# Gate-and-up block product: weight sums made by adding transfers from GpSimd's queue, and every channel tile finished in its own stage

## The chip, the cores and the metric

One core of one Trainium2 chip runs the whole program. The metric is device time in microseconds of one launch. PE is TensorE (PEld its weight loads), DVE VectorE, ACT ScalarE, POOL GpSimd, SP SyncE; L12 is line 12 of the kernel.

## The reference

One layer of a diffusion step on 128 context rows and 1024 latent rows (1152 in all) of width 1024, in float32: a normalised and modulated input, an input projection, an HGRN2 scan and an RWKV-7 scan in two directions, an output projection, then a gated feed-forward part whose gate is convolved over the grid:

```python
def block(x, mod, s_hgrn, s_rwkv, ffn_conv_fn, p):
    ...
    x = x + gate1 * (jnp.concatenate([o_a, o_b], axis=-1) @ p['w_out'])
    h = rmsnorm(x, p['norm_ffn_w']) * (1 + scale2) + shift2
    gt = ffn_conv_fn(h @ p['ffn_w_gate']) + p['ffn_conv_b']
    x = x + gate2 * ((jax.nn.gelu(gt) * (h @ p['ffn_w_up'])) @ p['ffn_w_down'])
```

The gate and up weights are 1024 x 2816 each (22 channel tiles of 128), the down weight 2816 x 1024. The convolution is 3 x 3 over the latent grid and 3 wide over the context.

## The kernel before, in words

**Precision.** Every large product is made of three passes of the fast float32 format: a float32 operand is split into a high part (a cast on ACT) and a low part (a subtraction on DVE, which reads the high part), and PE adds high x high, high x low and low x high (`split`, `product`, `three`).

**Stages.** First norms, transposes and the modulation; then input projections, the two scans and the output projection, mixed; then the gate-and-up products with the convolution (`weights`, `front`, `ffn_front`, `ffn_mid`); then the down projection in two halves of eleven channel tiles each (`ffn_down`), the first half starting from channel tiles 0 to 10, the second from 11 to 21.

**The block product.** For a channel tile, gate and up together are one matrix product of 2 x 2 blocks, done by seven block products instead of eight, in the manner of Strassen and Winograd. The seven left-hand blocks (`hq`) are made once from the activations. The seven weight blocks are made for each channel tile in `weights(ft)` from the four quarters b11, b21 (gate, upper and lower half of the rows) and b12, b22 (up): b11, b21, b11+b12+b22, b11+b12, b22+b12, b11+b12+b22+b21, b22. Four of them need an addition of 128 x 512 elements, on DVE into a tile `tq` (L2095, by `combine`). Each is then split into a pair `fwh`, `fwl` (L2090); there are four buffers of each. The activations stand in two groups, "a" (320 columns) and "b" (256), and each pair serves both; a block product is twelve matmuls (L2120). The results are collected in three PSUM tiles (`sy`, `sx`, `sz`) and put into the gate row `raw` and the up tile `u` (L2158 to L2179).

**Weight buffers.** The gate columns of a tile come into `wr` (512 KB, one buffer), the up columns into `fru` (512 KB, one buffer), both from SP's queue (L2085).

**The channel tile's middle.** `ffn_mid` runs the convolution: on ACT the middle tap and the activation function (L2203, L2204, L2213), on DVE eight taps of 1024 elements (L2209) and two of 128, then three products with `u`, and the result is stored to `d_a` (L2219).

**Tiles put off.** For the last five channel tiles (`NLATE = 5`) `raw` and `u` are stored to HBM instead (`d_gt`, `d_up`, L2241 and L2242). `late(j)`, called inside the first half of the down projection, loads them again (L2255, L2256) and runs `ffn_mid` there.

**What sets the order.** The kernel records every operation, and `Plan.schedule` then puts them into one order per engine by a list schedule: of the operations that are ready, the one with the longest way to the end is taken, plus its lead. The lead is a number for the function it was recorded in (`LEADS`) and one from the table `NUDGE`. A store may be put on POOL's queue or SP's (`st`, `either`), loads are on SP's (`ld`). Each engine then runs its instructions strictly in that order.

Of the kernel before, what the change touches and what calls it, by code (L numbers as in the profile page):

```python
# [20 lines left out]
P = 128  # L21
# [10 lines left out]
NLATE = 5  # L32
# [15 lines left out]
NUDGE = {1: 6, 3: -7, 4: -41, 5: -2, 7: 9, 8: 9, 9: 9, 10: 9, 11: 20, 12: 19, 13: 19, 14: 15, 15: 15, 16: 5, 17: -4, 18: -1, 19: -4, 20: -18, 21: -29, 22: -19, 23: -26, 24: -26, 25: -6, 27: -3, 28: -3, 29: -3, 30: -3, 31: -5, 32: -3, 33: -3, 35: -3, 51: -5, 52: -5, 53: -2, 84: -6, 85: -6, 86: -6, 87: -6, 88: 6, 91: -3, 92: -6, 93: -6, 94: -6, 95: -6, 96: -6, 97: -6, 98: -6, 104: -7, 105: -4, 108: -6, 109: 4, 110: -6, 111: -6, 119: 6, 127: -7, 140: 6, 141: 6, 142: 6, 143: 21, 144: 6, 145: 6, 147: -2, 172: -17, 173: -17, 174: -17, 175: -17, 183: -14, 184: -20, 185: -4, 189: 57, 190: 57, 191: 69, 193: 5, 194: 3, 200: -15, 201: -8, 203: 11, 204: 14, 206: 3, 212: -16, 217: 13, 218: 5, 224: -48, 225: -15, 226: -15, 227: -15, 236: 7, 239: -2, 243: -26, 244: -26, 245: -26, 246: -19, 247: -26, 251: 7, 252: 7, 253: 5, 254: -12, 266: -4, 269: 3, 275: 61, 282: -16, 290: -9, 292: 2, 294: 18, 295: 18, 296: 18, 297: 28, 298: 28, 299: 28, 300: 48, 301: 48, 302: 30, 303: 27, 305: 30, 306: 30, 307: 30, 308: 37, 309: 40, 310: 40, 311: 40, 312: 51, 313: 42, 314: 47, 315: 43, 316: 23, 317: 26, 318: 26, 319: 23, 320: 23, 321: 23, 322: 23, 323: 22, 328: 10, 329: 13, 330: 29, 331: 29, 337: -10, 338: -10, 339: -10, 340: -10, 341: -10, 342: -10, 343: -10, 344: 10, 345: 10, 346: 5, 347: 8, 348: 8, 349: 8, 350: 11, 351: 8, 352: -12, 353: -14, 354: -8, 355: -14, 356: 15, 357: -2, 358: 33, 359: 7, 360: -4, 361: 4, 362: -3, 363: -4, 364: 7, 365: -7, 367: 13, 368: 23, 370: 25, 377: 6, 378: 13, 379: 13, 380: 18, 381: 18, 382: 18, 390: 1, 396: 6, 398: 5, 400: -10, 401: -10, 404: -6, 405: -6, 406: -6, 407: -6, 408: -6, 409: -6, 410: -6, 411: -6, 412: -6, 413: -2, 416: -23, 417: 3, 418: 3, 419: 3, 425: -3, 426: -3, 427: -3, 428: -3, 453: -3, 454: -3, 455: -5, 456: 20, 457: 5, 458: 20, 459: 3, 460: -15, 461: 1, 462: -4, 463: -11, 464: -4, 465: -4, 466: -4, 467: -4, 468: -4, 469: -2, 470: 32, 471: 15, 472: 15, 473: 16, 474: 1, 475: 1, 476: 15, 477: 10, 478: 14, 479: 15, 480: 28, 481: 10, 482: 12, 483: 34, 484: 24, 485: 26, 486: 6, 487: 21, 488: 6, 489: 11, 490: 20, 491: 13, 492: 25, 493: 2, 494: -16, 495: -5, 496: -5, 497: -5, 498: -5, 499: -43, 500: -20, 501: -18, 502: -16, 503: -39, 504: -13, 505: -12, 506: -12, 507: -15, 508: -36, 509: -37, 510: -24, 511: -24, 512: -38, 516: 21, 517: 22, 518: 22, 519: 11, 520: 11, 521: 11, 522: 1, 523: 11, 524: 1, 525: 11, 526: 9, 527: 26, 528: -1, 529: 1, 530: -5, 532: -34, 533: -34, 534: -26, 535: -27, 536: 8, 537: 22, 538: 22, 539: 45, 540: 16, 541: 18, 542: 14, 543: 14, 544: 4, 545: 13, 546: 4, 547: 4, 548: 53, 549: 39, 550: 39, 551: 52}  # L48
# [129 lines left out]
class Plan:  # L178
# [3 lines left out]
    HELPERS = ("mm", "st", "copy", "combine", "split", "load_w", "record", "either")  # L182
# [7 lines left out]
    def __init__(self, tc, base):  # L190
        nc = tc.nc
        self.base = {F32: base, F32R: base.bitcast(F32R), I32: base.bitcast(I32)}
        self.tc = tc
        self.units = {"PE": nc.tensor, "DVE": nc.vector, "ACT": nc.scalar, "POOL": nc.gpsimd, "SP": nc.sync}
        self.ops, self.tags, self.tiles = [], {}, [None]
        self.live, self.group, self.chain_end, self.lead, self.boxes = {}, None, {}, 0.0, []
        self.first, self.mark = None, 0
        Plan.last = self
# [81 lines left out]
    @staticmethod  # L280
    def operands(m, args, kw):

        isap = lambda x: isinstance(x, AP)
        w = [args[0]]
        r = [x for x in args[1:] if isap(x)]
        for k, x in kw.items():
            if isap(x):
                (w if k == "accum_out" else r).append(x)
        if (m == "matmul" and not kw.get("start", True)) or m == "copy_predicated":
            r.append(args[0])  # L290
        return w, r
# [34 lines left out]
    def close(self, forms, room=()):  # L326
# [51 lines left out]
        op.place, op.dense, op.lead, op.kind = None, False, self.lead + LEADS.get(self.kind, 0.0) + NUDGE.get(op.id // 16, 0), self.kind  # L378
# [11 lines left out]
        return op  # L390

# [50 lines left out]
    def cost(self, e, l):  # L442
# [11 lines left out]
        if m == "dma_start":  # L454
            return .45 if len(a[0].ap) < 3 and len(a[1].ap) < 3 else .68
# [363 lines left out]
def step_kernel(ctx: ExitStack, tc: tile.TileContext, I, O):  # L819
# [8 lines left out]

    tl = plan.tile
# [101 lines left out]
    Layout(hbm, 0, 10240).add("qb1", 1024, 10)  # L931
    for t, box in (("fwh", "wh"), ("fwl", "wl")):
        plan.tag(t, [(m, 512 * b) for m, _ in plan.tags[box].places for b in range(2)], 512)
# [7 lines left out]
    Layout(low, 4944, 9198).add("u2", T).add("araw", 1408)  # L941
# [224 lines left out]
    gtd = dram("d_gt", [NLATE, P, 1320])  # L1166
    upd = dram("d_up", [NLATE, P, T])
# [912 lines left out]
    def weights(ft):  # L2080

        c = slice(ft * P, (ft + 1) * P)
        wg, wu = tl("wr", [P, KT, P]), tl("fru", [P, KT, P])
        for w, n in ((wg, "gate"), (wu, "up")):
            ld(w, I["ffn_w_" + n][0][:, c].rearrange("(a p) n -> p a n", p=P))  # L2085
        b11, b21, b12, b22 = wg[:, 0:4], wg[:, 4:8], wu[:, 0:4], wu[:, 4:8]
# [6 lines left out]
        def total(a, b):  # L2093
            t = tl("tq", [P, 4, P])
            combine(t, a, b, ADD)  # L2095
            return t

        yield pair(b11)
        yield pair(b21)
        t1 = total(b11, b12)  # L2100
        t2 = total(t1, b22)
        yield pair(t2)
        yield pair(t1)
        yield pair(total(b22, b12))
        yield pair(total(t2, b21))
        yield pair(b22)
# [45 lines left out]
    def front(sb, raw, us):  # L2152
# [13 lines left out]
        for dst, c in gate_places(raw, sb, 0):  # L2166
            dve.tensor_tensor(dst, like(dst, x[:, c]), like(dst, keep[1][:, c]), ADD)
        product(2, (yield), y, sb, False)
        save(2)
        z = pbank("sz")  # L2170
        product(3, (yield), z, sb, True)
# [49 lines left out]
    for ft in range(NFT):  # L2221
# [16 lines left out]
        if ft < NFT - NLATE:  # L2238
            ffn_mid(ft, raw, us[0])
        else:  # L2240
            st(gtd[ft - NFT + NLATE], raw)  # L2241
            st(upd[ft - NFT + NLATE], us[0])  # L2242

# [6 lines left out]

    def late(j):

        ft = NFT - NLATE + j
        raw, u = graws[ft % 2], tl("u2", [P, T])
        ld(raw, gtd[j])  # L2255
        ld(u, upd[j])  # L2256
        ffn_mid(ft, raw, u)
# [67 lines left out]
    def ffn_down(half):  # L2325
# [9 lines left out]
        for k in ks:  # L2335
# [8 lines left out]
            if half == 0 and k % 2 and k // 2 < NLATE - 1:  # L2344
                late(k // 2)
        for j, i in enumerate(head):
            finish(half, i, dn[j], fnw)
        for i in rest:
# [11 lines left out]
            if half == 0 and i == 3:  # L2360
                late(NLATE - 1)
# [34 lines left out]
```

## Time and profile before

| what | us |
|---|---|
| time, median of 3 runs | 1822.85 (1821.17 to 1830.99) |
| span of the profiled execution | 1818.9 |
| PE busy | 1768.3 (97%) |
| DVE busy | 1415.1 (78%) |
| ACT busy | 862.0 (47%) |
| POOL busy | 289.3 (16%) |
| DMA, mean | 169 GB/s, 307.45 MB |

The profile is of one execution; the median of the runs is 3.95 us above its span. A row of the wait list says who waited for whom, the total in us, how often, and the longest. In a list of lines by form, the number after the bar is the busy time, then the mean in ns, then the idle time just before and what ended it. "Landing" is the time from the issue of a transfer to its last completion count.

### The profile page before, as it was taken

The numbers are of one execution on the slowest core, as the hardware profiler recorded it, in microseconds if no ns is written. First come the engines' busy times: TensorE is split into PE (matmuls) and PEld (weight loads), VectorE is DVE, ScalarE is ACT, GpSimd is POOL, SyncE is SP. The second block draws the span as 40 slices with busy tenths as digits, with TensorE's granted clock in tenths as the row PEclk, the third lists the DMA queues.
The fourth block names the chain that finished last, engine by engine and source line by source line (L and its number), as shares of the span: only waits on it lengthen the run. The fifth ranks groups of instructions, "written<-read, shape, count | busy, mean of one in ns | idle before, by whom it ended". The sixth has DMA issues, their size and how long they took to land.

```text
span 1818.9 us, 45180 instructions
## 1 busy us (share of the span) xinstructions
PE 1768.3 (97%) x18402; PEld 1587.1 (87%) x18402; DVE 1415.1 (78%) x2670; ACT 862.0 (47%) x1753; POOL 289.3 (16%) x553
## 2 busy tenths in 40 slices
PE   7999999999999999999999999999999999999998
PEld 5889888899888788888788799999999999888887
DVE  7559899887778888876867889999999954985543
ACT  6556656543255645643636754444444433321321
POOL 2013435353312222122110100000000000000000
PEclk9999999999999999999999999999999999999999
DMA  9325637487757568889967522222222247774451
GB/s 325 102 72 151 147 102 180 128 229 193 207 165 246 165 203 258 267 283 306 324 207 244 203 59 73 73 73 73 73 73 73 76 126 251 227 272 162 133 169 67
DMA packets 272176, 307.45 MB, mean 169 GB/s; under 512 B 62611, under 2 KB 216849, under 8 KB 271968
## 3 DMA queue, kind: packets, MB, share of 16 engines
q1 hardware_dynamic: 245584, 224.33, 41.3%
q0 software_dynamic: 26384, 80.23, 13.1%
q8 instruction: 144, 2.36, 0.5%
q14 instruction: 64, 0.52, 0.1%
HBM read 200.50 MB, written 103.99 MB: 167 GB/s over the span
## 4 chain that ended last, share of the span: by engine, by line
PE 69%; DMA 5%; DVE 3%; ACT 1%; issue 1%; POOL 0%; SPq 0%; DVEq 0%; ACTq 0%; POOLq 0%
PE banks L2120 27%; PE banks L2269 5%; PE banks L2270 5%; PE banks L2271 5%; PE banks L1125 3%; PE banks L1127 3%; PE banks L1126 3%; DMA low<-d_ak 2%; PE banks L2011 2%; PE banks L2013 2%; PE banks L2012 2%; PE banks L1776 1%; PE banks L1827 1%; PE banks L1846 1%; PE banks L1646 1%
## 5 line engine op out<-in xcount | busy, mean ns | idle before, releaser
L1125 PE MATMUL banks<-hh,wh 128*128 128x384 f32 x768 | 282.0, 367 | 0.7 <-DVE fx L1314 0.7
L1127 PE MATMUL banks<-hh,wl 128*128 128x384 f32 x768 | 259.0, 337 | 0.0
L1126 PE MATMUL banks<-hl,wh 128*128 128x384 f32 x768 | 258.7, 337 | 0.0
L2209 DVE SCALAR_TENSOR_TENSOR low<-low,pf 128x1024 f32<-128x1024 f32 x176 | 224.8, 1279 | 4.6 <-ACT low L2203 3.0
L2120 PE MATMUL banks<-qm,wh 128*128 128x320 f32 x968 | 223.3, 310 | 0.0
L2120 PE MATMUL banks<-hbm,wh 128*128 128x256 f32 x880 | 164.4, 283 | 1.3 <-ACT low L1991 1.3
L1125 PEld LDWEIGHTS banks<-hh,wh 128*128 128x128 f32 x768 | 144.9, 189 | 21.0 <-issue 11.4
L2120 PE MATMUL banks<-qm,wl 128*128 128x320 f32 x528 | 162.8, 308 | 0.0
L2120 PEld LDWEIGHTS banks<-qm,wh 128*128 128x128 f32 x968 | 160.7, 189 | 0.1
L1126 PEld LDWEIGHTS banks<-hl,wh 128*128 128x128 f32 x768 | 145.5, 189 | 2.4 <-issue 1.2
L1127 PEld LDWEIGHTS banks<-hh,wl 128*128 128x128 f32 x768 | 145.0, 189 | 0.0
L2120 PEld LDWEIGHTS banks<-hbm,wh 128*128 128x128 f32 x880 | 140.4, 191 | 1.7 <-ACT low L1991 1.7
L2120 PE MATMUL banks<-ham,wh 128*128 128x256 f32 (+1 forms) x616 | 132.4, 295 | 0.0
L2120 PE MATMUL banks<-hbm,wl 128*128 128x256 f32 x440 | 124.8, 284 | 0.0
L2120 PEld LDWEIGHTS banks<-ham,wh 128*128 128x128 f32 x616 | 102.2, 192 | 0.0
L2120 PEld LDWEIGHTS banks<-qm,wl 128*128 128x128 f32 x528 | 99.1, 188 | 0.0
L2269 PE MATMUL banks<-qm,hbm 128*128 128x512 f32 (+1 forms) x240 | 93.7, 390 | 0.0
L2270 PE MATMUL banks<-qm,hbm 128*128 128x512 f32 (+1 forms) x240 | 93.6, 390 | 0.0
L2271 PE MATMUL banks<-qm,hbm 128*128 128x512 f32 (+1 forms) x240 | 93.5, 390 | 0.0
L2090 ACT CAST wh<-fx 128x512 fp32r<-128x512 f32 x88 | 54.3, 620 | 80.6 <-PE banks L2120 76.0
L2158 ACT COPY fx<-banks 128x320 f32<-128x320 f32 (+1 forms) x132 | 52.0, 397 | 84.2 <-PE banks L2120 82.8
L2120 PEld LDWEIGHTS banks<-hbm,wl 128*128 128x128 f32 x440 | 84.4, 192 | 0.0
(527 smaller groups left out, 4333.5 us busy)
## 6 DMA issues: line engine op xcount, KB each, us to landing
wr<-in_w_in_dram SPq DMA_DIRECT2D x34, 512.0 KB, 5.6
d_a<-low POOLq DMA_DIRECT2D x22, 576.0 KB, 3.4
low<-d_ak SPq DMA_DIRECT2D x64, 192.0 KB, 4.4
low<-in_ffn_w_up_dram SPq DMA_DIRECT2D x22, 512.0 KB
wr<-in_ffn_w_gate_dram SPq DMA_DIRECT2D x22, 512.0 KB, 3.7
low<-d_kb SPq DMA_DIRECT2D x36, 256.0 KB, 5.3
low<-d_a SPq DMA_DIRECT2D x12, 704.0 KB, 4.6
low<-in_ada_w_dram SPq DMA_DIRECT2D x32, 256.0 KB, 6.0
```

Of the source, the lines that this page charges most:

```text
L1125: mm(o, wh[:, kt, :], hh[:, kt, c], kt == 0, False)
L1126: mm(o, wh[:, kt, :], hl[:, kt, c], False, False)
L1127: mm(o, wl[:, kt, :], hh[:, kt, c], False, kt == KT - 1)
L2011: mm(ps, oh[:, kt, :], woh, kt == 0, False)
L2012: mm(ps, oh[:, kt, :], wol, False, False)
L2090: split(*w, src)
L2120: pe.matmul(o, a[:, kt, :], b[:, kt, :], start=start and first, stop=last, skip_group_check=not start)
L2158: act.copy(keep[n], y[:, 0:w])
L2209: dve.scalar_tensor_tensor(av, shifted(dy, dx), tap(3 * dy + dx), av, MUL, ADD)
L2269: mm(o, lh, w[:, 0, c], first, False)
L2270: mm(o, lh, w[:, 1, c], False, False)
L2271: mm(o, ll, w[:, 0, c], False, last)
```

## The change

It does three things.

1. `weights(ft)` loads the four quarters one by one (256 KB each, tag `fw`, four buffers: two in `wr`, two in `fru`). The sums are not made on DVE any more: a transfer issued from POOL's queue adds a quarter from HBM onto a buffer in place (`acc`, with `accum_op=ADD`). One buffer t holds b11, then b11+b12, then b11+b12+b22, then b11+b12+b22+b21, and is split between the additions; a second, t3, holds b12+b22. Products 2 and 3 change places, because b11+b12 now exists before b11+b12+b22.
2. `NLATE`, `late`, `d_gt` and `d_up` are gone: all 22 channel tiles run `ffn_mid` right after their product.
3. The table `NUDGE` is drawn anew, and is looked up by function and by the count of that function's operations instead of by the operation's number.

```diff
-NLATE = 5
...
-NUDGE = {1: 6, 3: -7, 4: -41, ...}
+NUDGE = {'step_kernel': [1, 8, 104, ...], 'const': [102], ...}
...
-        if (m == "matmul" and not kw.get("start", True)) or m == "copy_predicated":
+        if (m == "matmul" and not kw.get("start", True)) or m == "copy_predicated" or "accum_op" in kw:
...
-... self.lead + LEADS.get(self.kind, 0.0) + NUDGE.get(op.id // 16, 0), self.kind
+... self.lead + LEADS.get(self.kind, 0.0) + self.nudge(self.kind), self.kind
...
+    def acc(out, src):
+        pool.dma_start(out, src, accum_op=ADD)
...
+    fru = plan.tags["fru"].places[0][1]
+    plan.tag("fw", [(plan.tags["wr"].places[0][0], 512 * b) for b in range(2)] + [(low, fru + 512 * b) for b in range(2)], 512)
...
-        wg, wu = tl("wr", [P, KT, P]), tl("fru", [P, KT, P])
-        for w, n in ((wg, "gate"), (wu, "up")):
-            ld(w, I["ffn_w_" + n][0][:, c].rearrange("(a p) n -> p a n", p=P))
-        b11, b21, b12, b22 = wg[:, 0:4], wg[:, 4:8], wu[:, 0:4], wu[:, 4:8]
+        quarter = lambda n, h: I["ffn_w_" + n][0][512 * h:512 * h + 512, c].rearrange("(a p) n -> p a n", p=P)
+        b11, b21, b12, b22 = quarter("gate", 0), quarter("gate", 1), quarter("up", 0), quarter("up", 1)
+        def fetch(src):
+            w = tl("fw", [P, 4, P])
+            ld(w, src)
+            return w
...
-        def total(a, b):
-            t = tl("tq", [P, 4, P])
-            combine(t, a, b, ADD)
-            return t
-        yield pair(b11)
-        yield pair(b21)
-        t1 = total(b11, b12)
-        t2 = total(t1, b22)
-        yield pair(t2)
-        yield pair(t1)
-        yield pair(total(b22, b12))
-        yield pair(total(t2, b21))
-        yield pair(b22)
+        t = fetch(b11)
+        yield pair(t)
+        acc(t, b12)
+        yield pair(fetch(b21))
+        yield pair(t)
+        acc(t, b22)
+        t3 = fetch(b12)
+        acc(t3, b22)
+        yield pair(t)
+        acc(t, b21)
+        yield pair(t3)
+        yield pair(t)
+        yield pair(fetch(b22))
...
+        z = pbank("sz")
+        product(3, (yield), z, sb, True)
         product(2, (yield), y, sb, False)
         save(2)
-        z = pbank("sz")
-        product(3, (yield), z, sb, True)
...
-        if ft < NFT - NLATE:
-            ffn_mid(ft, raw, us[0])
-        else:
-            st(gtd[ft - NFT + NLATE], raw)
-            st(upd[ft - NFT + NLATE], us[0])
+        ffn_mid(ft, raw, us[0])
...
-            if half == 0 and k % 2 and k // 2 < NLATE - 1:
-                late(k // 2)
...
-            if half == 0 and i == 3:
-                late(NLATE - 1)
```

Three places in the order. The new kernel's line numbers are 11 to 13 higher around here (the products are L2133 there, the transposes L2036, the splits L2104, the taps L2222, the store of a finished tile L2232), and 1 higher in the down projection.

POOL in the gate-and-up stage, before: stores alone (d_a is a finished tile, d_gt and d_up one that is put off).

```order
L2110 MEMSET low 128x1320
L2219 DMA d_a<-low 128x1152 x16
L2241 DMA d_gt<-low 128x1320
L2242 DMA d_up<-low 128x1152
L2219 DMA d_a<-low 128x1152
L2241 DMA d_gt<-low 128x1320
```

POOL in the same stage now, some five tiles into it: L2109, L2112 and L2116 are the three additions onto t, L2114 the one onto t3.

```order
L2109 DMA low<-in_ffn_w_up_dram 128x4x128
L2114 DMA wr<-in_ffn_w_up_dram 128x4x128
L2112 DMA low<-in_ffn_w_up_dram 128x4x128
L2116 DMA low<-in_ffn_w_gate_dram 128x4x128
L2109 DMA low<-in_ffn_w_up_dram 128x4x128
L2114 DMA low<-in_ffn_w_up_dram 128x4x128
L2232 DMA d_a<-low 128x1152
L2112 DMA low<-in_ffn_w_up_dram 128x4x128
L2116 DMA low<-in_ffn_w_gate_dram 128x4x128
L2109 DMA wr<-in_ffn_w_up_dram 128x4x128
```

A queue of stores has become a queue of additions, four per tile, and of the 22 stores of finished tiles 12 stay between them while 10 are on SP's queue.

PE where the products of the second group begin, before: the transposes are of the last two row tiles (0 and 7), wh and wl are the weight pairs, qm holds left-hand blocks of group "a", ham and hbm those of "b".

```order
L2120 MATMUL banks<-qm,wh_131 128x320 x2
L2120 MATMUL banks<-qm,wl_133 128x320
L2025 MATMUL banks<-c_ident,low 128x128 x8
L2120 MATMUL banks<-qm,wh_131 128x320 x2
L2120 MATMUL banks<-qm,wl_133 128x320
L2025 MATMUL banks<-c_ident,low 128x128 x8
L2120 MATMUL banks<-hbm,wh_131 128x256 x2
L2120 MATMUL banks<-hbm,wl_133 128x256
L2120 MATMUL banks<-hbm,wh_131 128x256 x2
```

PE at the same place now:

```order
L2133 MATMUL banks<-qm,wh_130 128x320 x2
L2133 MATMUL banks<-qm,wl_132 128x320
L2036 MATMUL banks<-c_ident,low 128x128 x16
L2133 MATMUL banks<-ham,wh_129 128x256 x2
L2133 MATMUL banks<-ham,wl_131 128x256
L2133 MATMUL banks<-ham,wh_129 128x256 x2
L2133 MATMUL banks<-ham,wl_131 128x256
L2133 MATMUL banks<-qm,wh_130 128x320 x2
L2133 MATMUL banks<-qm,wl_132 128x320
```

The sixteen transposes stand together, the first product of group "b" is with the block on ham (blocks 0 and 1, of which block 0 is split as it is) and no longer with one on hbm (blocks 2 to 6), and products of group "a" are left to stand between those of "b".

DVE in the middle of the gate-and-up stage, before: L2090 is the second half of a split, L2095 a sum, L2209 a tap, L2174 and L2179 take results from PSUM.

```order
L2090 TENSOR_TENSOR wl_134<-wr,wh_132 128x512
L2090 TENSOR_TENSOR wl_133<-wr,wh_131 128x512
L2209 SCALAR_TENSOR_TENSOR low<-low,pf 128x1024
L2095 TENSOR_TENSOR fx<-wr,low 128x512
L2095 TENSOR_TENSOR fx<-fx,low 128x512
L2174 TENSOR_TENSOR low<-banks,fx 128x256
L2209 SCALAR_TENSOR_TENSOR low<-low,pf 128x1024
L2090 TENSOR_TENSOR wl_134<-fx,wh_132 128x512
```

DVE in the same stage now: L2104 is the second half of a split, L2222 a tap, L2180 and L2192 take results from PSUM.

```order
L2104 TENSOR_TENSOR wl_132<-low,wh_130 128x512
L2222 SCALAR_TENSOR_TENSOR low<-low,pf 128x1024 x3
L2180 TENSOR_TENSOR low<-banks,fx 128x4x64
L2180 TENSOR_TENSOR low<-banks,fx 128x64
L2180 TENSOR_TENSOR low<-banks,fx 128x4x64
L2222 SCALAR_TENSOR_TENSOR low<-low,pf 128x1024
L2104 TENSOR_TENSOR wl_131<-low,wh_129 128x512
L2192 TENSOR_TENSOR low<-banks,fx 128x320
L2192 TENSOR_TENSOR low<-banks,fx 128x256
L2104 TENSOR_TENSOR wl_131<-low,wh_129 128x512
L2222 SCALAR_TENSOR_TENSOR low<-low,pf 128x1024 x4
L2104 TENSOR_TENSOR wl_132<-low,wh_130 128x512
```

The sums are gone, and the taps stand in runs of three and four with a split behind each run.

More of the change, by code (lines that the diff above doesn't have):

```diff
@@ L181 @@
     PIECES = ("proj", "small_proj", "norm_rows", "modulate", "gate_rows", "load_step", "load_values", "conv_tiles")
-    HELPERS = ("mm", "st", "copy", "combine", "split", "load_w", "record", "either")
+    HELPERS = ("mm", "st", "copy", "combine", "split", "load_w", "record", "either", "acc", "fetch")
     ENGINES = ("PE", "DVE", "ACT", "POOL", "SP")
@@ L196, in __init__ @@
         self.live, self.group, self.chain_end, self.lead, self.boxes = {}, None, {}, 0.0, []
-        self.first, self.mark = None, 0
+        self.first, self.mark, self.seen = None, 0, {}
         Plan.last = self
@@ L377, in close @@
             self.tiles[v][3] += 1
-        op.place, op.dense, op.lead, op.kind = None, False, self.lead + LEADS.get(self.kind, 0.0) + NUDGE.get(op.id // 16, 0), self.kind
+        op.place, op.dense, op.lead, op.kind = None, False, self.lead + LEADS.get(self.kind, 0.0) + self.nudge(self.kind), self.kind
         op.table = None
@@ L390, in close, with nudge @@
         return op
+    def nudge(self, kind):
+        i = self.seen[kind] = self.seen.get(kind, -1) + 1
+        x = NUDGE.get(kind, ())
+        return x[i // 16] if i // 16 < len(x) else 0
     def follow(self, name):
@@ L454, in cost @@
         if m == "dma_start":
+            if "accum_op" in k:
+                return 1.0
             return .45 if len(a[0].ap) < 3 and len(a[1].ap) < 3 else .68
@@ L940, in step_kernel @@
     Layout(hbm, 4096, 10240).add("ak", 768, 3)
-    Layout(low, 4944, 9198).add("u2", T).add("araw", 1408)
+    Layout(low, 4944, 9198).add("araw", 1408)
     plan.tag("wdr", [plan.tags["wr"].places[0], (low, 7504)], 1024)
@@ L1165, in step_kernel @@
     actd = dram("d_a", [NFT, P, T])
-    gtd = dram("d_gt", [NLATE, P, 1320])
-    upd = dram("d_up", [NLATE, P, T])
     fd = dram("d_f", [NT, P, 1024])
@@ L2249, in gate_row @@
         gates.append(g)
[L2251 to L2257, printed above, removed]
     def down_weights(k):
```

2 lines of the change are left out of this document (1 added, 1 removed).

## The prediction

> **What bounds the kernel now.** I read the page's head first, then a table of busy time by stage, then the chain of waits and TensorE's own waits, and last the lines of the gate-and-up stage by form.
>
> The table by stage: start, recurrences and input projections (in three stretches), the block products, the down projection, the tail. The columns are the stretch, its length, and the busy time of PE, weight loads, DVE, ACT and POOL with the counts; then granted clock, DMA share and GB/s.
>
> ```profile
> span 1818.9 us, 45180 instructions
> ...
> 0.00:50.00 50.00, 37.70 (x288) 26.77 (x289) 37.15 (x117) 34.04 (x72) 12.33 (x40) 0.97 0.94 303
> 50.00:480.00 430.00, 423.58 (x4379) 381.81 (x4379) 346.58 (x698) 228.49 (x451) 147.42 (x267) 1.00 0.55 147
> 480.00:950.00 470.00, 451.72 (x8303) 388.84 (x8302) 366.85 (x883) 246.38 (x557) 97.84 (x190) 0.99 0.79 245
> 950.00:1049.00 99.00, 92.13 (x569) 77.48 (x567) 77.94 (x146) 65.85 (x146) 8.68 (x15) 0.98 0.61 208
> 1049.00:1536.70 487.70, 487.70 (x3649) 487.68 (x3650) 415.76 (x626) 212.17 (x415) 15.02 (x27) 0.99 0.28 89
> 1536.70:1812.20 275.50, 275.50 (x1221) 224.53 (x1219) 169.01 (x199) 73.52 (x109) 7.96 (x15) 1.00 0.54 179
> 1812.20:1818.90 6.70, 0.01 (x1) 0.00 (x0) 1.77 (x5) 1.52 (x4) 0.00 (x0) 0.76 0.21 78
> ```
>
> PE is busy for all of 487.70 us of the block products and all of the 275.50 us of the down projection, at a clock of 0.99 to 1.00. Only the first 1049 us have holes in PE: 12.3 us up to 50, then 6.4, 18.3 and 6.9, which is 31.6 us after the first 50. The tail has 6.7.
>
> The chain of waits around the start of the products, in order of time (start, length, what):
>
> ```profile
> 1033.95 6.60 PE banks L2120 x45
> 1040.56 0.89 PE banks L2025 x8
> ...
> 1044.98 0.61 DVE fx L2057
> 1045.62 1.13 PE banks L2025 x4
> ...
> 1048.90 487.76 PE banks L2120 x3648
> ```
>
> From 1048.90 on, 487.76 us of products stand in the chain as one piece: nothing but PE's own pace. TensorE's waits confirm it; the first row is of the stretch 950 to 1049, the second the only one after 1049:
>
> ```profile
> PE banks L2025 <- DVE fx L2057: 3.8, 1, 3.8
> PE banks L2120 <- ACT low L1991: 1.3, 1, 1.3
> ```
>
> So the change touches most in the two stages (763 us) in which there is no hole to close.
>
> **The change part by part.** The 0.5% that a measurement of this kernel can tell from no change is 9.1 us. The sum is made against the profiled span of 1818.9 us; the median of the runs, 1822.85, lies 3.95 above it, and I add that again at the end.
>
> *Vector work of the weight sums.* Lines of the product stage (1049 to 1536): count, busy us, mean ns, idle before.
>
> ```profile
> L2209 DVE SCALAR_TENSOR_TENSOR low<-low,pf 128x1024 f32<-128x1024 f32 x136 | 173.8, 1279 | 2.0 <-ACT low L2203 0.9
> ...
> L2090 ACT CAST wh<-fx 128x512 fp32r<-128x512 f32 x86 | 53.2, 620 | 80.6 <-PE banks L2120 76.0 <-issue 2.1 <-DVE low L2211 0.9
> ...
> L2095 DVE TENSOR_TENSOR fx<-fx,wr 128x512 f32<-128x512 f32 x22 | 15.0, 683 | 0.0
> L2095 DVE TENSOR_TENSOR fx<-low 128x512 f32<-128x512 f32 x22 | 15.0, 683 | 0.0
> L2095 DVE TENSOR_TENSOR fx<-fx,low 128x512 f32<-128x512 f32 x21 | 14.5, 689 | 0.6
> L2095 DVE TENSOR_TENSOR fx<-wr,low 128x512 f32<-128x512 f32 x21 | 14.3, 683 | 2.0 <-DMA low<-in_ffn_w_up_dram 2.0
> ```
>
> The four L2095 rows go: 58.8 us of DVE. The five channel tiles that were put off come back into this stage; their eight taps alone are 8 x 1.279 = 10.2 us per tile, 51 us for five. DVE stays near its 415.76 of 487.70, and PE's 487.70 does not move: the products are the same 22 x 7 x 2 x 12 = 3696. I cost both at nothing for the time; the cover is PE's unbroken work, and if it were gone DVE would still have 15% of the stage free. In the down stage DVE loses those 51 us of 169.01, also behind a full PE: nothing.
>
> *The transfers of the put-off tiles* go, stores and loads:
>
> ```profile
> d_gt<-low POOLq DMA_DIRECT2D x5, 660.0 KB, 3.3
> ...
> low<-d_up SPq DMA_DIRECT2D x5, 576.0 KB, 5.1
> ```
>
> They ran beside PE's full stages, so nothing again; the queues there were at a DMA share of 0.28 and 0.54.
>
> *The adding transfers.* This is what could cost. Per channel tile one buffer now carries b11, then b11+b12, then +b22, then +b21, and each addition can only be issued when the split of the value before it has been read by both ACT and DVE. The weight-pair buffers hold four pairs, and ACT waits 76.0 of its 80.6 us before the casts for PE to free one (row above), so pair k is split at the earliest when pair k-4 has been multiplied: three pair-times ahead of its own turn. A pair-time is 487.76 / (22 x 7) = 3.17 us. From the earliest split of pair 0 to the turn of pair 5, which needs the third addition, are 8 pair-times = 25.3 us. Less the last split, that leaves 24.0 us for three rounds of split, issue, landing: 8.0 us each. What a split takes, from one in the middle of the stage (start, length):
>
> ```profile
> 1223.53 0.62 ACT L2090 CAST wh<-fx 128x512 fp32r<-128x512 f32 x1 [1.31 <-PE banks L2120]
> ...
> 1224.18 0.69 DVE L2090 TENSOR_TENSOR wl<-fx,wh 128x512 fp32r<-128x512 f32 x1 [0.44 <-ACT wh L2090]
> ```
>
> From 1223.53 to 1224.87: 1.34 us. Add 0.3 for two hand-overs, an estimate from gaps such as the 0.03 between this cast's end and the subtraction, with room. No adding transfer is in this trace. Its nearest rows are POOL's plain transfers in pieces of 512 B (line 1484, 768 pieces; line 1423, up to 384) and the weight loads of the stage itself:
>
> ```profile
> L1484 POOL DMA_DIRECT2D d_ak<-top x10: 772/840/871, 130.5 to 363.2; - x10
> ...
> DMA to landing us min/median/max: 3.2/4.0/6.5
> L1423 POOL DMA_DIRECT2D d_v<-top x22: 567/760/785, 123.6 to 369.5; - x22
> ...
> DMA to landing us min/median/max: 2.5/3.9/5.8
> wr<-in_ffn_w_gate_dram SPq DMA_DIRECT2D x22, 512.0 KB, 3.7
> ```
>
> An addition has 512 such pieces and reads both operands, so from issue to landing I bound it by 2.5 and 6.5 and take 4.0: the 512 KB load of this quiet stage took 3.7, and I add 0.3 because POOL's issue alone is 0.8. A round is then 1.34 + 0.3 + 4.0 = 5.64, three are 16.9 of 24.0 us, and 7.1 us per tile are left for waiting in queues. Cost: nothing. The limit on the landing is 8.0 - 1.64 = 6.4, near the upper bound; beyond it PE stalls in each of 21 tiles. The slack of 7.1 has takers. In the order of DVE a split now stands behind runs of three or four taps, up to 4 x 1.279 = 5.1 us. On POOL a store of a finished tile (line 2232 in the new kernel) stands between additions, and the additions queued behind it wait until DVE has finished that tile; before, that queue held only stores.
>
> A rule that speaks against it: the Trainium skill, SBUF — State Buffer, section "SBUF: two separate sides", says that GpSimd cannot write its descriptors while VectorE runs an operation in a 2-port mode, so that transfers issued there stand still. The row first:
>
> ```profile
> L2219 POOL DMA_DIRECT2D d_a<-low x22: 531/531/533, 1091.0 to 1655.5; - x22
> ```
>
> All 22 stores were issued in 531 to 533 ns while DVE was 85% busy with two-operand operations, so no lock shows on the issue, and I charge nothing. By the Trainium skill's pair of figures there (620 ns alone, 3100 ns beside a copy) an addition would take about 2.5 us more, an estimate from that page alone.
>
> *SP's queue.* Two loads of 512 KB per tile become four of 256 KB, and each third or fourth waits for an addition chain to release its buffer. The 44 more issues lie in a queue that has little else in this stage: nothing.
>
> *The start of the products.* From 1040.56 to 1048.90 PE does 12 transposes and waits twice, 3.8 + 1.3 us. In the new order all 16 transposes stand together, and the first product of the second group is on ham (the block that is only cast, not subtracted first), where it was on hbm. The subtraction of line 2057 that ended the 3.8 is then not ahead of it, and the totals no longer share that tile's buffers. Between 0 and -5.1; I take -3.
>
> *The order set anew.* Every instruction before 1049 may stand elsewhere; the work on PE there is the same. What an order can return is PE's visible idle time after the first 50 us, less the 5.1 just used: 26.5. It can as well add holes of the same size, and the modelled ends of short matmuls hide more of either. For a gain speak the chain's transfers:
>
> ```profile
> PE 69%; DMA 5%; DVE 3%; ACT 1%; issue 1%; POOL 0%; SPq 0%; DVEq 0%; ACTq 0%; POOLq 0%
> ```
>
> 5% of 1818.9 is 91 us in which the chain stood in transfers that an order can start earlier, and seven copies fewer stand on DVE, the busier of the two vector engines. Bounds -26 and +26; I take -8, about a third of the visible idle time, for want of a nearer row.
>
> Sum: 0 + 0 + 0 - 3 - 8 = -11 on the span, 1808; with the 3.95 around it **1812 us**.
>
> **The rivals.** *Nothing to tell:* the additions are hidden, the new order gains in one place what it loses in another. For it: PE is 96% busy even from 480 to 950, and the number of products, transposes and projections is unchanged. 1822.85 - 3 = 1820.
>
> *The addition chain is the bound (slower).* One mechanism: a round passes 8.0 us. With the landing at its upper row, 6.5, and half a tap (0.64) in front of each split, a round is 1.34 + 0.3 + 6.5 + 0.64 = 8.78, three are 26.3, and 2.3 us are missing per tile; 21 tiles make 48 us, and 1812 + 48 = 1860. It decides from a landing of 6.4 with no queueing, of 5.7 with that half tap. For it: the splits behind runs of taps. Against it: 3.7 us for twice the bytes in the same stage.
>
> *The new order loses.* The holes between 480 and 950 double: 1820 + 18.3 = 1838. For it: there a matmul starts every 57 ns (8303 in 470 us) and four engines hand over between them, where a moved row upsets most.
>
> *The lock on descriptors decides.* If each addition's descriptors wait out two taps, 2 x 1.279 = 2.56, a round is 8.20, three are 24.6, 0.6 too much; 21 tiles make 13 us, 1812 + 13 = 1825. The 531 to 533 speak against it. This is the rule of the Trainium skill's SBUF — State Buffer above.
>
> **How the numbers follow.** Forecast (faster, about 1812): 0.44. Nothing to tell: 0.28. Lock: 0.03, also within 9.1 us of the median. Addition chain: 0.15. Order loses: 0.10. So faster by over 0.5% 0.44, within 0.5% 0.31, slower 0.25. The low end lets the order give nearly all of the visible idle time on top of the start: 1822.85 - 5 - 26 = 1792, and some of the hidden waits, 1786. The high end holds the losing order and the milder half of the addition chain, 1846; left out are some 6% below and 12% above. The forecast's own range is 1795 to 1814.
>
> **What would show it.** Right: from the first unbroken product on, again about 488 us to the down stage and 275 us after, no wait of PE for a cast of the weights (line 2104 in the new kernel); a landing of the additions under 5 us; DVE about 85% busy in the products; the hole between the transposes and the products under 5 us; PE's other idle time before it smaller by some 8. Wrong: waits of PE products on line 2104 that recur in each tile, POOL rows in which additions stand behind a store, a product stage over 500 us; or a first product that comes later than 1033.95 us.

## The result and the profile after

The changed kernel takes 1827.75 us, median of 20 runs (1821.6 to 1836.76), the kernel before 1821.2 us beside it (20 runs, 1815.34 to 1830.99). The ratio is 1.0032, 95% interval 1.0021 to 1.0043: slower by 0.3%, 5.8 us (the medians lie 6.6 us apart, the means 5.9). That is small but clear of the scatter: within the 0.5% that the prediction calls no change, and on the other side of the forecast of 1812 us.

The profiled execution is the fastest of the 20, so it shows less of a loss than a usual one has. The page of the changed kernel:

```profile
span 1819.7 us, 45360 instructions
...
PE 1767.6 (97%) x18402; PEld 1579.3 (87%) x18402; DVE 1361.8 (75%) x2577; ACT 858.4 (47%) x1757; POOL 391.8 (22%) x622
...
q0 software_dynamic: 70032, 91.46, 21.7%
```

The table by stage, same columns as before:

```profile
50.00:480.00 430.00, 424.32 (x4387) 382.66 (x4386) 342.88 (x690) 235.12 (x465) 149.16 (x268) 1.00 0.55 147
480.00:950.00 470.00, 453.81 (x8325) 389.21 (x8324) 369.32 (x888) 243.49 (x553) 94.85 (x186) 1.00 0.79 245
950.00:1049.00 99.00, 93.14 (x594) 78.62 (x593) 80.03 (x149) 67.14 (x149) 15.62 (x22) 1.00 0.73 226
1049.00:1536.70 487.70, 482.93 (x3588) 478.29 (x3588) 406.89 (x584) 212.64 (x415) 113.91 (x95) 1.00 0.62 123
1536.70:1812.20 275.50, 275.50 (x1233) 225.46 (x1233) 124.30 (x150) 63.57 (x99) 5.95 (x11) 1.00 0.46 151
```

In the products PE is busy for 482.93 of 487.70 us, where it was busy all the time. Ahead of them its holes went from 31.6 to 27.7 us (5.68 + 16.19 + 5.86). POOL's busy time in the products rose from 15.02 to 113.91 us. The chain of waits no longer runs through the products in one piece. Its last break, in order of time:

```profile
1432.78 4.80 DMA wr<-in_ffn_w_gate_dram
1437.65 0.48 issue
1438.13 1.14 ACT wh L2104 x2
1439.26 0.28 ACT fx L2171
1439.58 95.25 PE banks L2133 x711
```

Read it upwards: PE waited for an evacuation (L2171), which stood on ACT behind two casts of weights (L2104), which waited for an adding transfer of 4.80 us. TensorE's waits between 1049 and 1536.7 say how often:

```profile
PE banks L2133 <- ACT wh L2104: 1.9, 2, 1.3
PE banks L2133 <- DVE wl L2104: 1.4, 6, 0.6
PE banks L2133 <- ACT fx L2171: 1.2, 3, 0.9
PE banks L2133 <- DVE low L2192: 0.2, 1, 0.2
```

Twelve waits, 4.7 us; before, the only one was the 1.3 us that ended as this stretch began. What an addition costs (line 2109, the first of the four in each tile; then line 2114, the one into b12):

```profile
L2109 POOL DMA_DIRECT2D low<-in_ffn_w_up_dram x15: 1258/1277/1290, 1026.3 to 1508.7; - x15
...
DMA to landing us min/median/max: 4.5/4.8/6.9
```

```profile
L2114 POOL DMA_DIRECT2D low<-in_ffn_w_up_dram x14: 1258/1273/1819, 1049.8 to 1485.9; - x14
...
DMA to landing us min/median/max: 4.4/6.8/8.5
```

1.28 us of POOL for the issue and 4.8 us from its start to the landing; 6.8 in line 2114, which mostly follows another addition in the queue. One full round into a hole, from the order of time:

```profile
1402.02 1.27 POOL L2112 DMA_DIRECT2D low<-in_ffn_w_up_dram  x1 [4.88 <-DVE wl L2104]
1402.60 0.34 SPq L2232 DMA_DIRECT2D d_a<-low  x1
1409.18 1.14 ACT L2104 CAST wh<-low 128x512 fp32r<-128x512 f32 x2 [3.34 <-DMA low<-in_ffn_w_up_dram]
1409.84 1.29 DVE L2104 TENSOR_TENSOR wl<-low,wh 128x512 fp32r<-128x512 f32 x2 [1.81 <-ACT wh L2104]
...
1409.86 0.56 PE L2133 MATMUL banks<-qm,wh 128*128 128x320 f32 x2 [1.27 <-ACT wh L2104]
...
1410.82 1.29 POOL L2116 DMA_DIRECT2D low<-in_ffn_w_gate_dram  x1 [7.53 <-DVE wl L2104]
```

From the second addition to the third are 8.80 us, over the 8.0 that the prediction gives a round. 0.58 us after the addition, SP issues the store of a finished tile, and the addition lands after about 7.1 us.

### The profile page after: what moved, and what is told of

It is laid out like the page before. It is cut to its first block, busy times and chain, and to the rows that moved or that the text cites. A ratio compares the mean times of both kernels' runs of the same rounds, so it can differ in the third digit from the quotient of the medians.

```text
span 1819.7 us, 45360 instructions
## 1 busy us (share of the span) xinstructions
PE 1767.6 (97%) x18402; PEld 1579.3 (87%) x18402; DVE 1361.8 (75%) x2577; ACT 858.4 (47%) x1757; POOL 391.8 (22%) x622
## 3 DMA queue, kind: packets, MB, share of 16 engines
q0 software_dynamic: 70032, 91.46, 21.7%
## 5 line engine op out<-in xcount | busy, mean ns | idle before, releaser
L2222 DVE SCALAR_TENSOR_TENSOR low<-low,pf 128x1024 f32<-128x1024 f32 x176 | 225.6, 1282 | 14.2 <-ACT low L2216 11.0
L2133 PE MATMUL banks<-qm,wh 128*128 128x320 f32 x968 | 224.6, 311 | 4.2 <-ACT fx L2171 2.2
L2133 PEld LDWEIGHTS banks<-qm,wh 128*128 128x128 f32 x968 | 160.7, 189 | 6.6 <-ACT fx L2171 3.1
L2133 PE MATMUL banks<-qm,wl 128*128 128x320 f32 x528 | 163.5, 310 | 1.4 <-DVE wl L2104 1.4
L2133 PE MATMUL banks<-hbm,wh 128*128 128x256 f32 x880 | 162.8, 282 | 0.4 <-DVE low L2192 0.2
L2133 PEld LDWEIGHTS banks<-hbm,wh 128*128 128x128 f32 x880 | 139.1, 190 | 1.2 <-ACT fx L2171 0.7
L2133 PE MATMUL banks<-ham,wh 128*128 128x256 f32 (+1 forms) x616 | 131.5, 294 | 0.0
L2133 PE MATMUL banks<-hbm,wl 128*128 128x256 f32 x440 | 124.2, 282 | 0.0
L2171 ACT COPY fx<-banks 128x256 f32<-128x256 f32 (+1 forms) x132 | 51.7, 397 | 114.1 <-PE banks L2133 113.8
L2133 PEld LDWEIGHTS banks<-qm,wl 128*128 128x128 f32 x528 | 99.1, 188 | 3.0 <-DVE wl L2104 3.0
L2133 PEld LDWEIGHTS banks<-ham,wh 128*128 128x128 f32 x616 | 101.3, 189 | 0.2 <-ACT hbm L2064 0.2
L2104 ACT CAST wh<-low 128x512 fp32r<-128x512 f32 x89 | 54.6, 620 | 79.7 <-DMA low<-in_ffn_w_up_dram 42.2
L2270 PE MATMUL banks<-qm,hbm 128*128 128x512 f32 (+1 forms) x221 | 86.4, 391 | 0.0
L2271 PE MATMUL banks<-qm,hbm 128*128 128x512 f32 (+1 forms) x221 | 86.3, 391 | 0.0
L2272 PE MATMUL banks<-qm,hbm 128*128 128x512 f32 (+1 forms) x221 | 86.2, 390 | 0.0
L2133 PEld LDWEIGHTS banks<-hbm,wl 128*128 128x128 f32 x440 | 83.8, 190 | 0.0
```

The costliest lines, as they stand in the source:

```text
L2104: split(*w, src)
L2133: pe.matmul(o, a[:, kt, :], b[:, kt, :], start=start and first, stop=last, skip_group_check=not start)
L2171: act.copy(keep[n], y[:, 0:w])
L2222: dve.scalar_tensor_tensor(av, shifted(dy, dx), tap(3 * dy + dx), av, MUL, ADD)
L2270: mm(o, lh, w[:, 0, c], first, False)
L2271: mm(o, lh, w[:, 1, c], False, False)
```

## The experiments

Ratios are to the kernel before on the same chip. Where PE's time is read, three figures are used: the start of the first product, the time from there to the end of the span, and PE's idle time between 1060 and 1536 us. The last comes out too small, since the ends of matmuls are modelled. Counted by starts (all intervals of more than 0.26 us between starts of PE's instructions, less 0.14 us each), the holes behind 1060 are 7.5 us in the kernel after, where the row shows 4.8. The expectations speak of holes in this sense.

The theories at the start. T1: the chain of additions (issue, landing, split behind taps) stalls PE. T2: the new order costs it. T3: the five tiles taken back load DVE too much.

**1. The order alone, and the parts alone.** The first is the kernel before with the new table:

```diff
-NUDGE = {1: 6, 3: -7, ...}
+NUDGE = {'step_kernel': [1, 8, 104, ...], ...}
```

> The kernel before with the new table of shifts alone: sums on DVE, five channel tiles still put off. T1 (the chain of adding transfers stalls PE in the products and eats what the new order gives ahead of them): the first product about 4 us earlier and no new holes behind it, so 3 to 8 us below the kernel before, 1813 to 1818. T2 (the new order itself costs what was lost): as the kernel after, 1824 to 1830. T3 (taking the five tiles back on DVE in the products is what costs): as T1, 1813 to 1818.

The second is the kernel after with the old table, by number.

> The kernel after with the table of shifts of before: adding transfers and no tile put off, in an order that was set for the sums on DVE. T1: no earlier start, and the stalls behind the additions in full or more, 5 to 15 us above the kernel before, 1826 to 1836, with PE idle in the products behind casts and evacuations. T2: the parts cost nothing, so as the kernel before within 2 us, 1819 to 1823. T3: as T1 in time, but PE's waits in the products end on DVE's evacuations and subtractions and not on casts that waited for transfers.

Measured: 1885.66 us, ratio 1.0348 (1.0321 to 1.0374), and 1855.67 us, 1.0177 (1.0152 to 1.0202). Both lie outside everything that any theory expected. The program ahead of the products is the same in both kernels, yet the first product starts late:

```profile
L2126 PE MATMUL banks<-qm,wh x968: 303/310/637, 1057.8 to 1598.7; 128*128 128x320 f32 x194
```

```profile
L2133 PE MATMUL banks<-qm,wh x968: 304/310/494, 1047.3 to 1555.2; 128*128 128x320 f32 x194
```

1057.8 and 1047.3 against 1029.3 (the same table, kernel after) and 1033.8 (the same table, kernel before). Part of both losses is clock: the granted clocks of the runs have a mean of 0.985 and 0.990, against 0.994 of the kernel before, which is worth some 18 and 8 us as an estimate. The rest lies with the order. A list schedule ranks by the longest way to the end, so another product stage moves rows in the front as well, and a table of shifts belongs to the program it was made for. So the change can't be split into a part and an order by swapping tables; what follows therefore holds the order and changes the transfers.

**2. All additions plain, in the same order.** When the instruction is issued the sum is dropped; plan and order are those of after.

```diff
                 for m, a, k, line in l:
+                    k = {n: x for n, x in k.items() if n != "accum_op"}
```

> The kernel after in which every addition is a plain transfer of the same bytes in the same place of the same order: the sums of the weight blocks are left out, each transfer overwrites its buffer. T1: a plain transfer lands about 1 us sooner than an adding one (3.7 against 4.8 us) and is issued in less, so the stalls shrink: 4 to 8 us below the kernel after, 1819 to 1824. T2 and T3: as the kernel after within 2 us, 1825 to 1830.

Measured: 1819.97 us, 0.9993 (0.9971 to 1.0015). The kernel after, run again beside it:

> The kernel after unchanged, to have a second profile of it and its time beside the three others on the same chip. Every theory: 1.0032 times the kernel before within its interval, 1825 to 1830. T1: PE's holes from the first product to the end of the program sum to 8 to 16 us, more than in the first profile if this execution is a typical one, and they lie behind casts and evacuations on ACT.

Measured: 1825.64 us, 1.0029 (1.0006 to 1.0051). The mean of its 12 runs lies 6.9 us above that of the 12 runs with plain transfers, plus or minus 4.8: T1's size. Its second profile has holes by starts of 10.8 us from the first product to the end, in T1's range, but not more than the first profile's 11.5, as was expected. The line of the first transfer in the plain kernel:

```profile
L2110 POOL DMA_DIRECT2D low<-in_ffn_w_up_dram x15: 747/747/764, 1032.3 to 1505.4; - x15
...
DMA to landing us min/median/max: 3.3/3.6/5.6
```

The same bytes take 0.53 us less to issue and land 1.2 us sooner, counted from the start of the issue, without the sum. The stretch from 1060 to 1536 us in the kernel before, after, and with plain transfers:

```profile
1060.00:1536.00 476.00, 476.00 (x3577) 476.00 (x3576) 404.63 (x609) 203.90 (x399) 13.82 (x26) 1.00 0.28 90
```

```profile
1060.00:1536.00 476.00, 471.23 (x3501) 466.89 (x3500) 397.71 (x564) 206.94 (x402) 110.21 (x92) 1.00 0.62 122
```

```profile
1060.00:1536.00 476.00, 475.79 (x3562) 474.58 (x3561) 405.19 (x580) 210.98 (x408) 67.18 (x93) 1.00 0.42 126
```

PE's idle time: 0, 4.77 and 0.21 us. The five tiles taken back are in all of the last two, and with plain transfers PE has next to no hole, so T3 falls, and T2 falls for this stage.

**3. Which additions.** Only the addition into b12 plain (that sum is left out), then only the three of the chain through b11's buffer (those sums are left out):

```diff
+                    k = {n: x for n, x in k.items() if n != "accum_op" or line != 2115}
```

> The kernel after in the same order, with one of the four additions of each tile (into b12, for b12 + b22) as a plain transfer that overwrites its buffer: that sum is left out. Two theories on where the waits behind additions come from. M (they come where two additions meet in GpSimd's queue and the landing goes from 4.8 to about 7): without the meeting partner the other three land in 4.8 nearly always, the holes of PE behind weights between 1060 and 1560 shrink from 7 to below 3 us, 3 to 6 us below the kernel after, 1820 to 1825. L (each round of a lone addition, 1.27 + 3.5 us to landing beside splits and queues, is already at its limit): the holes stay at 5 to 7 us, time as the kernel after within 2 us.

```diff
+                    k = {n: x for n, x in k.items() if n != "accum_op" or line == 2115}
```

> The kernel after in the same order, with the three additions of the chain through b11's buffer as plain transfers, and the one into b12 still adding: the chain's sums are left out. M: one adding transfer per tile remains and meets plain ones; most of the gain of all four plain (7 us), 1818 to 1823. L: all of it, since the chain's own rounds are what is at the limit: 1818 to 1822, and no hole of PE behind weights between 1060 and 1560 above 1 us in all.

Measured: 1829.53 us, 1.0027 (1.0009 to 1.0045), and 1819.74 us, 0.9979 (0.9963 to 0.9996). One plain, then three plain:

```profile
1060.00:1536.00 476.00, 470.91 (x3506) 466.74 (x3504) 396.26 (x568) 204.01 (x399) 102.68 (x94) 1.00 0.57 121
```

```profile
1060.00:1536.00 476.00, 474.69 (x3554) 473.43 (x3554) 403.70 (x577) 210.41 (x407) 78.62 (x93) 1.00 0.47 125
```

Idle 5.09 and 1.31 us, by starts 7.7 and 1.8. L holds: that the partner in the queue adds (M) does not matter, though the landing of line 2114 looks bad; the chain's own rounds are the limit. The partner is still there as a plain transfer, so what its presence costs is not shown. L's "no hole above 1 us in all" was a little short.

**4. Why only some tiles: the stores.** The stores that the plan put on SP's queue near an addition go to POOL's queue behind it. The core of the edit:

```diff
+        for o in [o for o in ops if o.dma and o.kind == "ffn_mid" and o.forms[0][0] == "SP"]:
+            near = [x for x in adds if abs(o.start - x.start) < 1.5]
+            if near:
+                o.forms = [("POOL", o.forms[0][1])]
...
+                        self.order.insert(j, self.order.pop(i))
```

> The kernel after, in which the ten stores of finished tiles that the plan puts on SP's queue within 1.5 us of an addition go to GpSimd's queue, behind that addition where they stood ahead of it; every other engine's order is that of after, and PE's and DVE's and ACT's rows are the same. S (the long landings of 6.4 to 7.1 us in the tiles with holes come from a store of 576 KB that starts within 0.6 us of the addition, as at 1209.8, 1232.6 and 1402.0): those landings fall to 5 us or less, and the holes of PE behind weights between 1060 and 1560 from 7 to 3 to 5 us, 2 to 4 us below the kernel after, 1822 to 1826. Rival Q (the store takes the same wires wherever it stands, and now also 0.58 us of the queue in which the additions are issued): holes of 6 us or more, as the kernel after within 2 us or slower.

Measured: 1824.72 us, 1.0014 (0.9995 to 1.0033).

```profile
1060.00:1536.00 476.00, 473.68 (x3543) 471.40 (x3542) 400.31 (x575) 208.37 (x406) 119.60 (x105) 1.00 0.63 123
```

Idle 2.32 us against 4.77; the holes by starts are 3.6 us against 7.5, and no landing of the chain's additions that the trace records (26 of 66; 51 in the kernel after) is above 5.9 us, where the kernel after has 6.6, 6.4 and 7.1 beside a store. Of these three additions two are recorded here, with 4.6 and 5.2. The store holds up plain transfers as well: in the kernel of experiment 2 they take 5.6, 5.5 and 4.0 us in the same three places, against a median of 3.6. S holds for about half of the holes. The 3 us in the time are less than the two intervals together can tell; one profile of each shows them.

**5. The additions alone**, with the old table and the five tiles still put off.

```diff
 NLATE = 5
...
-        t1 = total(b11, b12)
+        acc(t, b12)
...
```

> The kernel before with its own table of shifts and five tiles put off, in which the weight sums alone are made by adding transfers; PE's order is that of before for 3785 of its 8793 rows. Measured by PE's time from the first product to its last matmul: 778.4 us in the kernel before, 783.3 after. T1 (an addition of 1.27 us issue and 4.8 us landing, longer where two meet in the queue, makes PE wait in some tiles): 784 to 795, with waits of products on casts and splits of the weights that total 5 us or more; whole time 1828 to 1850, as far as the order ahead is put out too. Rival R (additions are hidden; what the second run lost was an order that no longer fits): 776 to 781 and no such waits.

Measured: 1850.67 us, 1.0148 (1.0125 to 1.0171). First product to last matmul 793.2, inside T1's range, but with only 0.5 us of waits on splits behind 1060; the rest are evacuations and the start of the products. What the additions and what the new plan cost can't be told apart here: inconclusive.

**6. Sums on GpSimd instead of transfers.**

```diff
-            combine(t, a, b, ADD)
+            combine(t, a, b, ADD, ("POOL",))
```

> The kernel before with its four sums per channel tile as tensor_tensor on GpSimd, still out of loaded blocks; no adding transfer; PE's order is the same up to the first products. T1: nothing in the chain lands, so PE does not wait for the weights: first product to last matmul 776 to 781, whole time as the kernel before within 3 us, 1819 to 1826, DVE's busy time in the products lower by some 60 us. Rival (GpSimd's two-input sums hold up DVE's operations, so moving sums off DVE does not pay in any form): DVE's taps longer than 1.28 us, PE waits in the products, 1828 or more.

Measured: 1841.17 us, 1.0101 (1.0079 to 1.0123): the rival's time. DVE's lines in the products, and a sum on POOL:

```profile
L2209 DVE SCALAR_TENSOR_TENSOR low<-low,pf 128x1024 f32<-128x1024 f32 x136 | 197.5, 1452 | 2.9 <-ACT low L2203 1.3
...
L2090 DVE TENSOR_TENSOR wl<-wr,wh 128x512 fp32r<-128x512 f32 x42 | 44.6, 1068 | 17.2 <-ACT wh L2090 17.1
```

```profile
L2095 POOL TENSOR_TENSOR fx<-fx,wr 128x512 f32<-128x512 f32 x22 | 41.3, 1877 | 0.0
```

A tap takes 1452 ns instead of 1279, a split out of `wr` 1068 instead of 688 in the kernel before. DVE is rid of 58.8 us of sums and is still busy for 416.02 of 487.70 us, against 415.76 (1425.7 and 1415.1 in the whole execution): what was taken off comes back as longer times of its other instructions. Those that read one operand from PSUM keep their length (line 2167, 256 columns: 417 ns, before 418). The Trainium skill, SBUF — State Buffer, section "SBUF: two separate sides", says that a DVE instruction with two SBUF inputs and a GpSimd instruction that reads SBUF hold the shared ports by turns, each for its whole length; the trace agrees, by these lengths. Adding transfers do relieve DVE without this: its taps take 1282 ns in the kernel after.

**7. One sum taken out of the transfers.** b12 + b22 on GpSimd, and the same on DVE, out of two loaded blocks:

```diff
         t3 = fetch(b12)
-        acc(t3, b22)
+        r = fetch(b22)
+        add(t3, t3, r)
...
-        yield pair(fetch(b22))
+        yield pair(r)
```

> The kernel after in which one of the four additions (b12 + b22, the one that meets others in GpSimd's queue) is a tensor_tensor on GpSimd out of two loaded blocks; PE's order is that of after up to the first products. T1: the three additions left land alone (4.8 us instead of up to 8), the waits behind them shrink from about 7 to 3 us or less: 3 to 7 us below the kernel after, 1819 to 1824. Rival (the landing of a lone addition is already too long): as the kernel after within 2 us, 1824 to 1829.

> The kernel after in which b12 + b22 is summed on DVE out of two loaded blocks (22 sums of 0.69 us, 15 us on DVE), the three other additions stay; PE's order is that of after up to the first products. M: additions no longer meet, DVE's taps stay at 1.28 us: first product to last matmul 776 to 782, 0 to 6 us below the kernel after. L: 782 to 790 with waits behind casts as in the kernel after. An order that no longer fits (as with the sum on GpSimd, 793.5, where the taps also grew to 1.30): above 788 with waits on evacuations that no addition precedes.

Measured: 1837.84 us, 1.0081 (1.0054 to 1.0108), and 1840.35 us, 1.0099 (1.0080 to 1.0119). Neither gain came, and the first lies 9 us above its rival too. In the second, first product to last matmul is 793.6 us, and PE waits longest on evacuations, 7.0 us in seven waits: its last line, an order that no longer fits. By experiment 3 the sum in this transfer costs nothing that shows, so there was little to gain.

**8. A plan that knows the landing.**

```diff
-                return 1.0
+                return 1.27
...
+                if "accum_op" in op.forms[0][1][0][2]:
+                    op.end += 1.0
```

> The kernel after, planned with 1.27 us instead of 1.0 for the issue of an addition and 1 us more for its landing; nothing else differs, and PE's order is that of after for 4595 of 8798 rows. T1: an order that knows the long landings leaves fewer waits behind them: 2 to 6 us below the kernel after, 1820 to 1825, if the shifts of the table still fit. Rival (any new plan leaves the table's shifts unfit, as in the first two runs): 5 to 30 us above the kernel after, whatever the additions do.

Measured: 1871.89 us, 1.0272 (1.0241 to 1.0302): some 44 us above the kernel after, beyond even the rival's 30. A better number in the planner was worth nothing with a table made for the worse one.

**9. The kernel before once more**, for a second profile.

> The kernel before unchanged, for a second profile. Every theory: first product to last matmul 778 to 779, no waits of products on weights. If the new order brought nothing ahead of the products, the first product comes at 1031 to 1037, the range of the kernels in after's order so far (1028.8 to 1035.3); if the 4.5 us of the first pair of profiles were real, at 1033 or later.

Measured: 1819.65 us, first product at 1033.5, 784.4 us from there to the end, no idle time of PE from 1060 to 1536. It did not separate the two expectations by itself; with the other runs it does:

| kernel | first product | from there to the end of the span |
|---|---|---|
| before, twice | 1033.8, 1033.5 | 785.1, 784.4 |
| after, twice | 1029.3, 1028.8 | 790.4, 790.7 |
| one plain (order of after) | 1036.2 | 791.6 |
| four plain, three plain (order of after) | 1035.3, 1034.2 | 781.6, 783.8 |
| stores behind (order of after on PE, DVE, ACT) | 1039.4 | 786.3 |

Ahead of the first product the six executions in after's order lie between 1028.8 and 1039.4, mean 1033.9; before's two at 1033.8 and 1033.5. So the 4.5 us of the first pair of profiles are no gain of the order. Behind it, the two of after are 5.8 us longer than the two of before, as much as was measured.

These times hold one thing more, the granted clock. From the first product to 1060, before and after:

```profile
1033.80:1060.00 26.20, 21.14 (x134) 20.48 (x133) 23.22 (x44) 19.16 (x40) 1.74 (x2) 0.80 0.16 53
```

```profile
1029.30:1060.00 30.70, 27.26 (x199) 26.13 (x198) 25.96 (x52) 20.59 (x45) 6.84 (x6) 1.00 0.65 144
```

The clock was 0.80 in one and 1.00 in the other. At 1050, in the slow part (0.52 from 1045 to 1055), three matmuls of 256 columns take 0.64 us in the kernel before, and at 1056 they take 0.36. PE's busy time in the row times the missing part of the clock is an estimate of what it cost; behind 1060 the rows show 1.00 in all eight.

| kernel | clock, first product to 1060 | cost, estimate | behind the first product without it |
|---|---|---|---|
| before, twice | 0.80, 0.87 | 4.2, 2.8 | 780.9, 781.6 |
| after, twice | 1.00, 0.95 | 0, 1.4 | 790.4, 789.3 |
| one plain | 0.93 | 1.5 | 790.1 |
| four plain, three plain | 1.00, 0.93 | 0, 1.6 | 781.6, 782.2 |
| stores behind | 0.92 | 1.4 | 784.9 |

At one clock, then, the additions cost some 8 us (one execution with all four plain, two with them), and the kernel with plain transfers is as fast behind the first product as the kernel before: neither the new start nor the new order shows a gain there. Ahead of it the clock would explain most of the first pair's 4.5 us as well: in the kernel before it was 0.97 up to 50 us, 0.98 from 300 to 400 and 0.66 from 500 to 510, some 6 us by the same estimate, in the kernel after only 0.98 from 300 to 400, 2 us. The timed runs go the same way: on the chip of experiment 2 the mean clock was 0.9944 in 23 runs of the kernel before, 0.9961 in 12 of the kernel after and 0.9956 in 12 with plain transfers, which is worth 3 and 2 us. Why the clock is higher in the new order, no run shows.

No version here is shown to beat the kernel before with its sums in: stores behind comes nearest, at 1.0014.

## Why the prediction was wrong

**What bounds the kernel.** Right: PE's pace in the products and the down projection, and no hole there to close. The clock of 0.99 in the row of the products was read and then left out of the sum; experiment 9 shows that it differs between the kernels by about 3 us. The down projection again takes all of its 275.50 us, without the put-off tiles as with them.

**Vector work and the put-off tiles, at nothing.** Right. DVE is busy for 83% of the products (85% forecast), and with plain transfers the same five tiles leave PE without a hole.

**The adding transfers, "Cost: nothing".** This step failed. The mechanism stood in the text: a round of split, issue and landing, three of them, with a limit of 8.0 us each, and splits behind taps. The landing was taken at 4.0 us from a plain load of twice the bytes; it is 4.8 alone, because the sum costs 1.2 us over a plain transfer of the same bytes (0.53 of them in the issue), and 5.2 to 7.1 where SP starts a store of a finished tile within 0.6 us, three times above 6.4 (a fourth such landing, 6.9, follows another addition). A round is then 6.4 us with the 1.64 of split and hand-overs, and over 8.0 beside a store (8.80 above). The 7.1 us of slack per tile were an average, counted once for a chain whose rounds fail one by one. So the stall is neither zero nor in every tile: 7 to 8 us in all, by the run with plain transfers (6.9 between the means, 7.5 and 6.8 of holes by starts, 8 behind the first product at one clock). The rival "addition chain is the bound" named the mechanism at 48 us; it decides, at between a seventh and a sixth of its price. The text also looked for the store in the wrong place, in POOL's queue ahead of additions; it was on SP's, beside them.

**The lock on descriptors.** Rightly kept out. Additions are issued in 1258 to 1290 ns (line 2109) with DVE 83% busy, and the rule of the Trainium skill that the prediction cites (SBUF — State Buffer, "SBUF: two separate sides") shows nowhere in them. Whether any of DVE's instructions here runs in a 2-port mode, no run shows, so the rule itself was not put to the test.

**The start of the products, -3 of 0 to -5.1.** About half came as waits, none that shows as time. The stretch 950 to 1049 of the kernel after:

```profile
PE banks L2036 <- DVE low L2002: 2.3, 2, 1.3
...
PE banks L2133 <- ACT fx L2171: 1.2, 2, 0.7
```

3.5 us of waits instead of 5.1: -1.6. At one clock, the time behind the first product with plain transfers (781.6) is not below that of the kernel before (780.9 and 781.6).

**The order set anew, -8.** The second failed step. It had no row behind it but the size of the idle time. The first table of experiment 9 shows no gain ahead of the products; the 3.8 us in the first profile are within what executions of one order differ by, and no more than the clock differed by. The bounds of 26 us either way were no bounds at all: other plans of the same work cost 15 to 63 us.

**The sum as measured,** from the first product on: 0 for vector work and the transfers of put-off tiles, 8.3 for the additions (789.9 against 781.6), 0.3 for the start and the order together (781.6 against 781.3), and -2.8 for the clock (0.7 instead of 3.5), for which the prediction has no term. That these make 5.8 us follows from the way they are taken, but no other term is left to find. The waits alone, 7 less 1.6, come near it too; that is luck, since they leave out the clock. The range, 1786 to 1846, held the time.

## What to carry to other kernels

Price an adding transfer by its own landing and not by a plain one's, and check a chain of dependent transfers round by round against the turn at which each result is needed, with the other transfers that start in the same microsecond; a mean slack per tile hides the rounds that fail. Where a tuned list schedule stands between an edit and the engines, hold the order fixed and change what the instructions do; a new plan moves more than the edit. And compare several executions from the same landmark, each with its granted clock, before a few us in one profile are called a gain.

## What the runs showed of the hardware

- An addition of 256 KB in pieces of 512 B takes 1.27 us to issue and 4.8 us to land, counted from the start of the issue, the plain transfer in its place 0.75 and 3.6. The software queue counts 70032 packets instead of 30608 (with plain transfers, the row below) for the same 91.46 MB: the 88 additions add 448 each.

```profile
q0 software_dynamic: 30608, 91.46, 15.8%
```

- GpSimd takes 1.50 to 1.88 us for a float32 sum of 128 x 512 beside a busy DVE (0.68 on DVE), and makes DVE's two-input instructions 14 to 55% longer.
- In the start of the products the granted clock was 0.80 and 0.87 in the two executions of the kernel before, 1.00 and 0.95 in the two of the kernel after, and three matmuls of 256 columns took up to 0.64 us there instead of 0.36.
